# A recurrence's two heads in one row order, with the x term made ahead and the steps in a written order

## The chip, the cores and the metric

The kernel runs on one core of a Trainium2 chip. The metric is the device time of one execution in microseconds (us). Before the change, three executions took 2452.4, 2445.73 and 2456.51 us, so the median is 2452.4 us. The profile is of a further execution that took 2443.87 us.

Five engines work side by side, each through its own instructions in order: TensorE (PE in the profile, with its weight loads as PEld), VectorE (DVE), ScalarE (ACT), GpSimd (POOL) and SyncE (SP), which here does nothing but start DMAs. They wait for each other by semaphores.

## The reference, cut to what matters

One decoder block: RMSNorm, one input projection (1024 tokens, width 1024), a dilated attention branch and an RWKV-7 branch, a gated merge, an output projection, a SwiGLU feed-forward layer and a last RMSNorm. The change touches the RWKV-7 branch alone. It has 16 heads of 64 features and runs this recurrence over 1024 tokens:

```
def _rwkv7_step(state, inp):
    r_t, w_t, k_t, v_t, a_t, b_t = inp
    sa = jnp.einsum('bhvk,bhk->bhv', state, a_t)
    state = (state * w_t[:, :, None, :] + sa[..., None] * b_t[:, :, None, :]
             + v_t[..., None] * k_t[:, :, None, :])
    y = jnp.einsum('bhvk,bhk->bhv', state, r_t)
    return state, y
```

After it, y is normalized within each head, a bonus term is added, and the result is multiplied by a gate.

## The kernel before, in words

The recurrence is computed in chunks of L = 64 tokens. Within a chunk all products of two tokens come from one matmul and a triangular mask; a 64x64 triangular system is solved by the inverses of its 16x16 diagonal blocks; and only the state (64x64 per head) goes from chunk to chunk.

A **unit** is 256 tokens of four heads: 128 partitions hold two heads (rows 0 to 63 and 64 to 127), and the free axis holds two such pairs of 256 tokens, so a unit has NCH = 8 chunks, in two chains of four that advance together. There are 16 units. Each unit goes through:

- `rwkv_feat`: decay sums, their exponentials, normalized k.
- `rwkv_pre`: `ab` and `bk` (decayed operands); their products `pmg` (L730), masked on DVE into `aab` (L734) for one half of the rows, and copied by ACT (L736) and masked by POOL (L737) into `ab` for the other half; the first to memory and back, to fetch the diagonal blocks (`d1`, `a16`); v turned and copied twice, into `sv` and `uv` (L763, L764); the bonus; the block inverses on DVE (L786, L788), again to memory and back (`d2`, `cmp`), and spread by a mask multiply on POOL and DVE into `td` and `tdt` (L795); and then a row of small matmuls, each needing the last (`lvw` L807, `lvta`, `lvtt`, `lvw` L831, `lvt`), to the inverse `tt`.
- `rwkv_chain`: for each of four steps x (L868), u (L875) and the state update d (L887 on PE, L882 on POOL, four L891 on DVE), then the outputs `py`, and the normalization, gate and store.

The two heads of a pair use opposite row halves: a head's rows 0 to 63 hold its state and the other 64 its v, and the second head has them the other way round. So one 128-row matmul gives x with v's part in it:

```
T_.matmul(px[A, x, :], ab[:, cx, hh, 0, :], sv[:, cx, hh, :], start=True, stop=True)
```

All matmuls of the recurrence are small (64 or 32 columns, or 128) and on f32 operands; each stands as two records in the trace. The engine is kept fed between them by **filler**: the projection matmuls (L230, 128x512, one record each) of later heads' r, k, v and of the gates. `run` interleaves generators (chain, pre of the next unit, feat of the one after it, filler) by shares of a unit, one `yield` at a time. From that sequence, the compiler's list scheduler makes a fixed order for each engine, with durations that it assumes itself. What runs is this fixed order, and the waits in it are those of the chip.

Of the kernel before, what the change touches and what calls it, by code (L numbers as in the profile page):

```python
# [16 lines left out]
P = 128  # L17
S = 1024
# [8 lines left out]
NCH = HALF // L  # L27
NEG = -1.0e30
# [59 lines left out]
NV = 98  # L88

# [30 lines left out]
class K:  # L120
# [350 lines left out]
    def lora(self, sd, ad, gd):  # L471
# [9 lines left out]
        whh = sb.tile([P, 2, DM], F32R, tag="ab", name="whh", bufs=2)  # L481
# [52 lines left out]
    def rwkv(self, sd, ad, gd, ob, first, fill):  # L534

        nc, tc, a = self.nc, self.tc, self.a
        with ExitStack() as ctx:
# [17 lines left out]
            self.xm, self.svs, self.unit, self.feat = {}, {}, {}, {}  # L555
# [4 lines left out]
            run((chain_of([self.lora(sd, ad, gd), self.rwkv_gemm(0, "k"), self.rwkv_gemm(1, "k")]), 1, 0.0, 1.0))  # L560
            with tc.issue_after(self.last_sigmoid.ins):
                pre = nc.scalar.preload_act_table_set("natural_log_exp_and_others")
            with tc.issue_after(pre.ins):
                run((self.rwkv_feat(0, dd, "k"), 3, 0.1, 0.5), (self.rwkv_pre(0), 11, 0.6, 1.0), (self.rwkv_feat(1, dd), 3, 0.7, 1.0),
                    (chain_of([self.rwkv_gemm(0, "rv"), self.rwkv_gemm(1, "rv")]), 36, 0.0, 0.6),
                    (chain_of(gates(first)), 9 * len(first) + 1, 0.6, 1.0))
            later = [(q, x) for q in range(2, NPAIR) for x in "krv"]
            for n in range(N):
                ms = fill.get(n, ())

                k = 3 if n < 2 else 1 + n % 2
                f = [self.rwkv_gemm(*x) for x in later[:k]]
                later = later[k:]
                f += gates(ms)
                nf = 9 * len(f)
                jobs = [(self.rwkv_chain(n, gd, ob), 15, 0.0, 1.0)]
                if f:
                    jobs.append((chain_of(f), nf, 0.0, 1.0 if nf > 9 else 0.6))
                if n + 1 < N:
                    jobs.append((self.rwkv_pre(n + 1), 11, 0.0, 1.0))  # L580
                if n + 2 < N:
                    jobs.append((self.rwkv_feat(n + 2, dd), 3, 0.4, 1.0))
                run(*jobs)

    def rwkv_gemm(self, pr, kinds):
        nc, a, sb = self.nc, self.a, self.rb
        h = self.h
        for kind in kinds:
# [22 lines left out]
    def head_sums(self, src, nm):  # L611

# [4 lines left out]
        nc.vector.tensor_tensor(out=lo, in0=src, in1=hi, op=ALU.subtract)  # L617
        pss = self.rp.tile([P, HALF], F32, tag="st", name=f"pm{nm}", bufs=1)
# [15 lines left out]
    def block_of(self, d, n):  # L634

        pp, qd = n // 4, n % 4
        W = HALF // 2
        return d[2 * pp * P : (2 * pp + 2) * P, qd * W : (qd + 1) * W].rearrange("(x p) t -> p x t", x=2)

    def loaded(self, n, kinds):  # L640

        for x in kinds:
            t = self.xm[x, n] = self.rb.tile([P, HALF], F32, tag=f"xm{x}", name=f"xm{x}_{n}", bufs=2)
            self.nc.sync.dma_start(t.rearrange("p (x t) -> p x t", x=2), self.block_of(self.xd[x], n))

    def rwkv_feat(self, n, dd, kinds="krv"):

        nc, sb, ps = self.nc, self.rb, self.rp
        V, A_, T_ = nc.vector, nc.scalar, nc.tensor
        pp, qd = n // 4, n % 4  # L650
        nm = f"{pp}_{qd}"
        src = lambda d: self.block_of(d, n)
        f = lambda tag, bufs=1, shape=None: sb.tile(shape or [P, HALF], F32, tag=tag, name=f"{tag}_{nm}", bufs=bufs)
        pm = lambda n, shape=None: ps.tile(shape or [P, HALF], F32, tag="pm", name=f"pm{n}_{nm}", bufs=2)
        H0, H1 = slice(0, L), slice(L, P)
        heads = ((0, H0, H1), (1, H1, H0))
        col = lambda n, x: self.v(n, 2 * pp + x)
# [4 lines left out]
        xs = (slice(0, HALF // 2), slice(HALF // 2, HALF))  # L662
        halves = lambda t: t.rearrange("p (x t) -> p x t", x=2)
        nc.sync.dma_start(halves(sg), src(sd))
        nc.sync.dma_start(halves(at), src(ad))
# [14 lines left out]
        pss = self.head_sums(sq, f"ss_{nm}")  # L680
# [7 lines left out]
        for x, c in enumerate(xs):  # L688
            A_.activation(ka[:, c], at[:, c], AF.Identity, scale=col("k_a", x),
                          bias=self.oka[:, 2 * pp + x : 2 * pp + x + 1])  # L690
# [5 lines left out]
    def rwkv_pre(self, n):  # L696

        nc, sb, ps = self.nc, self.rb, self.rp
        V, A_, T_ = nc.vector, nc.scalar, nc.tensor
        pp, qd = n // 4, n % 4  # L700
        nm = f"{pp}_{qd}"
        src = lambda d: self.block_of(d, n)
# [3 lines left out]
        heads = ((0, H0, H1), (1, H1, H0))  # L706
        col = lambda n, x: self.v(n, 2 * pp + x)
        ch = lambda t: t.rearrange("p (c t) -> p c t", t=L)
        TT, STT, TS = V.tensor_tensor, V.scalar_tensor_tensor, V.tensor_scalar
        lv = lambda n, shape: ps.tile(shape, F32, tag="lv", name=f"lv{n}_{nm}", bufs=1)  # L710
# [3 lines left out]
        ab = f("ab", 2, [P, NCH, 2, 2, L])  # L714
        bk = f("bk", 1, [P, NCH, 2, L])
        for hh, A, _ in heads:
            STT(out=ab[A, :, hh, 0, :], in0=ch(kk)[A], scalar=-1.0, in1=pt[A, :, 0:L], op0=ALU.mult, op1=ALU.mult)
            TT(out=ab[A, :, hh, 1, :], in0=ch(r)[A], in1=pt[A, :, 1:], op=ALU.mult)
            TT(out=bk[A, :, hh, :], in0=ch(at)[A], in1=ch(pi)[A], op=ALU.mult)
            TT(out=bk[A, :, 1 - hh, :], in0=ch(k)[A], in1=ch(pi)[A], op=ALU.mult)  # L720

        yield

        aab = f("aab", 2, [P, NCH, 2, L])
        for q in range(2):
            q4 = slice(4 * q, 4 * q + 4)
            gs = [pm(f"g{q}{hh}", [P, 4, P]) for hh in range(2)]
            for j in range(4):
                for hh, A, _ in heads:
# [102 lines left out]
        for hh in range(2):  # L832
            A_.copy(w2[Q[2 * hh + 1]], pw[Q[2 * hh + 1]])
# [598 lines left out]
```

## Time and profile before

| | |
|---|---|
| median of three executions | 2452.4 us |
| profiled execution | 2443.87 us, of which the span of instructions is 2441.9 us |
| PE busy | 2331.3 us (95%) |
| DVE, ACT, POOL busy | 1600.6, 1202.7, 788.7 us |
| recurrence, 130 to 960 us after the start | 830 us, PE busy 775.03 us |

How to read it: busy time is the union of an engine's instructions, and matmuls overlap in the pipeline, so two matmuls that are 0.23 us apart can each be shown as 0.39 us long. The distance from start to start is what one costs. "Idle before" is the time the engine did nothing before an instruction, with the one that ended it. PEclk is the granted TensorE clock, where 1.00 is 2.4 GHz and half of it 1.2 GHz.

### The profile page before, as it was taken

The page shows a single profiled execution, that of the slowest core. Times are in us where ns is not written, and L with a number is a line of the kernel's source. Part 1 is how long each engine was busy: PE and PEld are TensorE (multiplying, and loading weights), DVE is VectorE, ACT ScalarE, POOL GpSimd, SP SyncE. Part 2 cuts the span into 40 slices and gives each one's busy share as a digit, 9 for nine tenths or more (in the row PEclk, how much of TensorE's full clock was granted, in tenths as well). Part 3 has the DMA queues.
Part 4 walks back from the last instruction along what each step waited for, and adds up shares of the span by engine and source line. Part 5 has one row for each costly group of instructions (what it writes and reads, how often), then busy time and mean ns, then how long its engine had stood idle before and what let it go on. Part 6 is the DMA issues. An engine that isn't in the chain of part 4 may idle for free. (4 is left out here: it accounts for less than half of the span.)

```text
span 2441.9 us, 40487 instructions
## 1 busy us (share of the span) xinstructions
PE 2331.3 (95%) x15102; PEld 1825.6 (75%) x15102; DVE 1600.6 (66%) x3251; ACT 1202.7 (49%) x2345; POOL 788.7 (32%) x689
## 2 busy tenths in 40 slices
PE   8999899999989999999999999999989999999998
PEld 5676677667666667777777777889968888887886
DVE  5267687888886773788888786342465555555656
ACT  7444455555445543677777775242233333334444
POOL 1133243334332432111111100023086777682200
PEclk9999999999999999999999999999989999999999
DMA  5642333323333322111111126453134444447555
GB/s 184 231 131 76 88 96 103 97 80 110 85 97 85 84 68 89 35 36 39 40 39 40 39 68 222 149 188 119 70 103 151 147 154 170 165 164 264 183 190 184
DMA packets 302532, 284.79 MB, mean 117 GB/s; under 512 B 82411, under 2 KB 226240, under 8 KB 302208
## 3 DMA queue, kind: packets, MB, share of 16 engines
q1 hardware_dynamic: 297856, 267.10, 34.9%
q0 software_dynamic: 4480, 15.12, 1.7%
q8 instruction: 118, 1.93, 0.3%
q14 instruction: 78, 0.64, 0.1%
HBM read 187.65 MB, written 92.54 MB: 115 GB/s over the span
## 5 line engine op out<-in xcount | busy, mean ns | idle before, releaser
L426 ACT CAST ph<-pt 128x512 fp32r<-128x512 f32 x192 | 89.8, 478 | 75.0 <-PE pt L423 74.4
L427 DVE TENSOR_TENSOR pl<-pt,ph 128x512 fp32r<-128x512 f32 x192 | 106.1, 554 | 31.3 <-ACT ph L426 29.9
L737 POOL TENSOR_TENSOR ab<-ab,gmask 64x512 f32<-64x512 f32 x64 | 91.3, 1427 | 105.4 <-ACT ab L736 100.1
L1315 PE MATMUL o<-dwlo,dfh 128*128 128x512 f32 x276 | 109.7, 398 | 2.9 <-DVE dwlo L1082 2.9
L423 PE MATMUL pt<-ident,pb 128*128 128x128 f32 x576 | 103.9, 277 | 8.0 <-DVE pb L400 5.6
L230 PE MATMUL pg_sg<-hhi,wh_sg 128*128 128x512 f32 x256 | 110.8, 433 | 0.0
L1315 PE MATMUL o<-dwhi,dfh 128*128 128x512 f32 x276 | 109.3, 396 | 1.5 <-ACT dwhi L1081 1.5
L882 POOL TENSOR_TENSOR s<-sv,pt 64x128 f32<-64x128 f32 x120 | 59.8, 498 | 153.8 <-DVE sv L891 144.2
L1315 PE MATMUL o<-dwhi,dfl 128*128 128x512 f32 x276 | 109.1, 395 | 0.0
L397 ACT ACTIVATE pb<-pb,mn 128x128 f32<-128x128 f32 (+7 forms) x128 | 99.2, 777 | 19.1 <-DVE mn L392 17.4
L1082 DVE TENSOR_TENSOR dfl<-fr,dfh 128x512 fp32r<-128x512 f32 x69 | 58.5, 851 | 71.9 <-ACT dfh L1081 71.7
L230 PE MATMUL pg_sg<-hhi,wl_sg 128*128 128x512 f32 x256 | 105.0, 410 | 0.0
L230 PE MATMUL pg_sg<-hlo,wh_sg 128*128 128x512 f32 x256 | 104.0, 406 | 0.0
L423 PEld LDWEIGHTS pt<-ident,pb 128*128 128x128 f32 x576 | 71.0, 141 | 36.9 <-DVE pb L400 8.8
L891 DVE SCALAR_TENSOR_TENSOR sv<-chd,pt,s 64x64 f32<-64x64 f32 x240 | 67.9, 283 | 41.2 <-PE chd L887 35.7
L1081 ACT CAST dfh<-fr 128x512 fp32r<-128x512 f32 x69 | 42.6, 618 | 97.7 <-PE o L1315 85.0
L209 POOL TENSOR_TENSOR wl_sg<-wr_sg,wh_sg 128x512 fp32r<-128x512 f32 x32 | 44.9, 1402 | 112.4 <-ACT wh_sg L208 106.5
L392 DVE CUSTOM_DVE_ANT_0 pb<-sc,nbias 128x512 f32<-128x512 f32 (+3 forms) x128 | 72.6, 585 | 7.7 <-PE sc L390 6.4
L1017 PE MATMUL wo<-wowoh,mhi 128*128 128x256 f32 x256 | 72.5, 284 | 1.0 <-DVE x L1020 1.0
L432 PE MATMUL po<-ph,vt 128*128 128x512 f32 x192 | 72.8, 383 | 0.4 <-ACT ph L426 0.3
L1017 PE MATMUL wo<-wowoh,mlo 128*128 128x256 f32 x256 | 72.5, 283 | 0.0
L1017 PE MATMUL wo<-wowol,mhi 128*128 128x256 f32 x256 | 72.3, 283 | 0.0
(502 smaller groups left out, 7578.1 us busy)
## 6 DMA issues: line engine op xcount, KB each, us to landing
fr<-fd SPq DMA_DIRECT2D x77, 256.0 KB
wd<-in_ffn_w_down_dram SPq DMA_DIRECT2D x11, 1024.0 KB
td<-wd SPq DMA_DIRECT2D x11, 1024.0 KB
wr<-td SPq DMA_DIRECT2D x44, 256.0 KB
wg<-in_ffn_w_gate_dram SPq DMA_DIRECT2D x10, 1024.0 KB
wu<-in_ffn_w_up_dram SPq DMA_DIRECT2D x10, 1024.0 KB
fd<-fs SPq DMA_DIRECT2D x40, 256.0 KB
wr<-in_ffn_w_down_dram SPq DMA_DIRECT2D x33, 256.0 KB
```

What stands on the lines that cost most here:

```text
L230: nc.tensor.matmul(pg, lw, rx[:, k, :], start=(i == 0), stop=(i == n - 1))
L392: nc.vector.tensor_tensor_reduce(out=pb[:, b * HALF : b * HALF + n], in0=sc[:, :n], in1=nbias[:, bo : bo + n], scale=1.0, scalar=(3.0e38 i ...
L397: nc.scalar.activation(pb[:, :nk], pb[:, :nk], AF.Exp, bias=last, scale=-1.0, accum_out=mn[:, 2:3])
L423: nc.tensor.transpose(pt[:, j * P : (j + 1) * P], probs[j][:, kb * P : (kb + 1) * P], self.ident)
L426: nc.scalar.copy(ph[:, c0:], pt[:, c0:])
L427: nc.vector.tensor_tensor(out=pl[:, c0:], in0=pt[:, c0:], in1=ph[:, c0:], op=ALU.subtract)
L432: nc.tensor.matmul(po[:, c0:], vt[:, b, hh, :], ph[:, c0:], start=(b == 0), stop=False)
L737: nc.gpsimd.tensor_tensor(out=dst, in0=dst, in1=m4[B], op=ALU.mult)
L882: nc.gpsimd.tensor_tensor(out=s2[A], in0=sv[A, c::NC, hh, :], in1=pt[A, c::NC, L : L + 1].broadcast_to([L, 2, L]), op=ALU.mult)
L891: STT(out=nsv[A, ncx, hh, :], in0=pd[A, x, :], scalar=pt[A, cx, L : L + 1], in1=s2[A, x, :], op0=ALU.mult, op1=ALU.add)
L1017: nc.tensor.matmul(pt, lw[:, k, ts_], rx[:, k, :], start=(n == 0), stop=(n == 3 * KT - 1))
L1315: T_.matmul(pt, lw[:, ts_], rx, start=(first and n == 0 and x == 0), stop=(last and x == 2), skip_group_check=True)
```

## The change

The row order becomes the same for both heads. g (all masked products) is kept on 128 partitions per head: b's rows in 0 to 63 and k's in 64 to 127, masked by one DVE instruction of 128 rows, and neither ACT nor POOL takes part. The state `st` is a tile of its own with head 0 in rows 0 to 63 and head 1 in the others. Hence:

- x is a 64-row matmul of the state alone; v's part of it, `xv`, is made ahead in `rwkv_pre` (16 small matmuls a unit, one ACT copy), and DVE adds it instead of ACT's copy of x.
- The old state enters the update as a matmul with the identity (16 a unit), and one DVE multiply by the decay ends it, in place of POOL's product and four DVE instructions.
- The block inverses go to memory straight into the places of a zeroed 64x64 layout (pieces of 64 bytes) and come back as `td` and `tdt`; the mask multiplies on POOL and DVE are gone. The masked products are also read back whole (`aa`). The zeroes are written once, by eight DMAs at the start.
- The bonus and the end of a unit become generators of their own, sums over heads are split in two (operands in one step, matmuls in the next), and `ALONG` says which of them advances after each of the 12 steps of a chain. The last step of `rwkv_pre` moves into the next unit.

The diff, cut to its core:

```
-                jobs = [(self.rwkv_chain(n, gd, ob), 15, 0.0, 1.0)]
...
+                run((self.unit_steps(n, own), 12, 0.0, 1.0), (chain_of(f), nf, 0.0, 1.0))
...
+    ALONG = (("last", "pre"), ("pre",), ("pre",), ("pre", "out"), ("out", "pre"), ("pre",), ("pre", "feat"),
+             ("pre", "feat"), ("feat",), ("pre", "feat"), ("pre", "bonus"), ("pre", "bonus"))
+    def unit_steps(self, n, own):
+        chain = self.rwkv_chain(n)
+        for along in self.ALONG:
+            next(chain, None)
+            for x in along:
+                if own[x] is not None:
+                    next(own[x], None)
+            yield
...
+                for i in range(2):
+                    flat = d[i].rearrange("(p f) -> p f", p=P)
+                    nc.sync.dma_start(flat[:, :HALF], zero)
+                    nc.sync.dma_start(flat[:, HALF:], zero[:, : flat.shape[1] - HALF])
...
-            for hh, A, B in heads:
-                TT(out=aab[A, q4].rearrange("p j i t -> p j (i t)"), in0=gs[hh][A], in1=m4[A], op=ALU.mult)
-                dst = ab[B, q4, hh].rearrange("p j i t -> p j (i t)")
-                A_.copy(dst, gs[hh][B])
-                nc.gpsimd.tensor_tensor(out=dst, in0=dst, in1=m4[B], op=ALU.mult)
+            for hh, A in heads:
+                TT(out=g[:, q4, hh].rearrange("p j i t -> p j (i t)"), in0=gs[hh], in1=m4, op=ALU.mult)
...
+        for hh, A in heads:
+            nc.sync.dma_start(aa[A], mats(d1)[hh].rearrange("c (s t) -> s c t", t=L))
...
-            for hh, _, B in heads:
-                A_.copy(sv[B, par::2, hh, :], pv[src, :, hh, :])
-                A_.copy(uv[B, par::2, hh, :], pv[src, :, hh, :])
+            A_.copy(uv[H1, par::2], pv[src])
...
+        for c in range(NCH):
+            for hh, A in heads:
+                T_.matmul(pv[A, c, :], g[H1, c, hh, 0, :], uv[H1, c, hh, :], start=True, stop=True)
+        A_.copy(xv, pv)
...
-        for i, (dst, eng) in enumerate(((td, nc.gpsimd), (tdt, nc.vector))):
-            cmp_ = f(f"cmp{i}", 1, [P, NCH, 16])
-            nc.sync.dma_start(cmp_, d2[i].rearrange("(c x) i j -> (x i) c j", c=NCH))
-            eng.tensor_tensor(out=dst, in0=cmp_.unsqueeze(2).broadcast_to([P, NCH, 4, 16]),
-                              in1=self.blk16.unsqueeze(1).unsqueeze(3).broadcast_to([P, NCH, 4, 16]), op=ALU.mult)
+        for i, dst in enumerate((td, tdt)):
+            nc.sync.dma_start(diag(d2[i]), tp[:, i])
+            m2 = mats(d2[i].rearrange("(c x) -> c x", c=NCH))
+            for hh, A in heads:
+                nc.sync.dma_start(dst[A], m2[hh].rearrange("c (s t) -> s c t", t=L))
...
-                    T_.matmul(px[A, x, :], ab[:, cx, hh, 0, :], sv[:, cx, hh, :], start=True, stop=True)
-            A_.copy(xt, px)
+                T_.matmul(px[A, x, :], ar[A, cx, 0, :], st[A, cx, :], start=True, stop=True)
+            V.tensor_tensor(out=xt, in0=px, in1=xv[:, c::NC, :], op=ALU.add)
...
-                        STT(out=nsv[A, ncx, hh, :], in0=pd[A, x, :], scalar=pt[A, cx, L : L + 1], in1=s2[A, x, :],
-                            op0=ALU.mult, op1=ALU.add)
+                    T_.matmul(pd[A, x, :], self.ident[:, A], st[:, cx, :], start=True, stop=False)
+                    T_.matmul(pd[A, x, :], bkt[:, cx, A], uv[:, cx, hh, :], start=False, stop=True)
+                nst, c1 = (st, c + 1) if c < NC - 1 else (self.svs[n + 1], 0)
+                V.tensor_tensor(out=nst[:, c1::NC, :], in0=pd,
+                                in1=pt[:, c::NC, L : L + 1].broadcast_to([P, UP, L]), op=ALU.mult)
```

In the engines' orders, three places show what moves. The first is PE's order around the first matmuls of the triangular solve of the third unit, `lvw` (names end in head pair and quarter; `pg_sv3` is filler). Before:

```order
L230 MATMUL pg_sv3_0_2632<-hlo0_169,wh_sv3_1_2628 128x512
L807 MATMUL lvw_0_2_2602<-td_0_2_2545,am_0_2_2599 64x64 x16
L230 MATMUL pg_sv3_0_2632<-hhi0_168,wl_sv3_1_2629 128x512
L230 MATMUL pg_sv3_0_2632<-hhi0_168,wh_sv3_1_2628 128x512
L230 MATMUL pg_sv3_0_2632<-hlo0_169,wh_sv3_1_2628 128x512
L230 MATMUL pg_sv3_0_2632<-hhi0_168,wl_sv3_1_2629 128x512
L230 MATMUL pg_sv3_1_2726<-hhi1_250,wh_sv3_0_2622 128x512
L816 MATMUL lvta_0_2_2653<-am_0_2_2599,tdt_0_2_2546 32x32 x16
```

And the same place of the changed kernel:

```order
L840 MATMUL lvw_0_2_2671<-td_332,am_0_2_2476 64x64
L239 MATMUL pg_sv3_1_2640<-hhi1_250,wh_sv3_0_2554 128x512
L239 MATMUL pg_sv3_1_2640<-hlo1_251,wh_sv3_0_2554 128x512
L239 MATMUL pg_sv3_1_2640<-hhi1_250,wl_sv3_0_2555 128x512
L239 MATMUL pg_sv3_1_2640<-hhi1_250,wh_sv3_1_2560 128x512
L239 MATMUL pg_sv3_1_2640<-hlo1_251,wh_sv3_1_2560 128x512
L239 MATMUL pg_sv3_1_2640<-hhi1_250,wl_sv3_1_2561 128x512
L239 MATMUL pg_sv3_1_2640<-hhi1_250,wh_sv3_1_2560 128x512
L840 MATMUL lvw_0_2_2671<-td_332,am_0_2_2476 64x64 x15
```

The 16 matmuls are split: the first stands alone, since it needs one of `td`'s two reads only, and seven filler matmuls stand ahead of the other 15.

The second is SP's order where a unit's block inverses (`t16`) go to memory and come back. Before:

```order
L205 DMA wr_sg4_1_7487<-in_w_in_dram 128x4x128
L790 DMA d2_2_1_6441<-t16_2_1_6575 64x2x256
L794 DMA cmp0_2_1_6613<-d2_2_1_6441 128x8x16
L794 DMA cmp1_2_1_6616<-d2_2_1_6441 128x8x16
L665 DMA at_3_0_7770<-ad_73 128x2x256
```

And of the changed kernel:

```order
L214 DMA wr_sg4_0_7371<-in_w_in_dram 128x4x128
L828 DMA d2_1_335<-t16_2_1_6478 64x16x16 x2
L831 DMA td_332<-d2_1_335 64x8x64 x2
L831 DMA tdt_333<-d2_1_335 64x8x64 x2
L643 DMA gates_75<-gt3_1_6693 128x512
```

One write and two reads become two writes (in pieces of 16 numbers) and four reads, back to back.

The third is DVE's order from a copy of u to the new state. Before, with the steps of the block inverses between:

```order
L786 TENSOR_TENSOR t16m_1_0_3705<-a16_1_0_3571,t16_1_0_3704 64x11x5
L891 SCALAR_TENSOR_TENSOR sv_0_3_3025<-chd2_0_3_3773,pt_0_3_2564,s2_0_3_3770 64x64
L788 TENSOR_TENSOR t16_1_0_3704<-t16_1_0_3704,t16m_1_0_3705 64x11x5
L891 SCALAR_TENSOR_TENSOR sv_0_3_3025<-chd2_0_3_3773,pt_0_3_2564,s2_0_3_3770 64x64
L786 TENSOR_TENSOR t16m_1_0_3705<-a16_1_0_3571,t16_1_0_3704 64x10x6
L891 SCALAR_TENSOR_TENSOR sv_0_3_3025<-chd2_0_3_3773,pt_0_3_2564,s2_0_3_3770 64x64
```

And of the changed kernel:

```order
L927 COPY uv_0_3_3027<-chu0_0_3_3452 64x2x64
L769 TENSOR_TENSOR g_1_0_3490<-pmg01_1_0_3492,gmask_319 128x4x128
L937 TENSOR_TENSOR st_0_3_3026<-chd0_0_3_3479,pt_0_3_2535 128x2x64
L920 TENSOR_TENSOR xt_0_3_3515<-chx1_0_3_3510,xv_0_3_3057 128x128
L769 TENSOR_TENSOR g_1_0_3490<-pmg10_1_0_3517,gmask_319 128x4x128
```

Four state instructions, with other work between them, become one; the sum that makes `xt` is new on this engine.

## Rows read from the trace of the kernel before

**Rows 1.** The page: the span, and PE's busy time.

```profile
span 2441.9 us, 40487 instructions
...
PE 2331.3 (95%) x15102; PEld 1825.6 (75%) x15102; DVE 1600.6 (66%) x3251; ACT 1202.7 (49%) x2345; POOL 788.7 (32%) x689
```

**Rows 2.** Busy time by stretch: length; PE, PEld, DVE, ACT, POOL; clock; DMA.

```profile
130.00:960.00 830.00, 775.03 (x7660) 568.51 (x7659) 636.06 (x1446) 411.30 (x867) 298.48 (x321) 0.98 0.33 91
960.00:1600.00 640.00, 620.96 (x3074) 496.18 (x3073) 464.90 (x1094) 413.51 (x825) 76.14 (x61) 0.99 0.24 75
```

**Rows 3.** What PE waited for, 130 to 960: total us, times, longest.

```profile
PE lvw L807 <- POOL td L795: 21.9, 12, 3.1
PE chu L875 <- ACT tt L840: 6.4, 4, 2.9
PE chx L868 <- DVE sv L891: 5.5, 10, 1.3
PE pmbk L769 <- ACT uv L764: 4.9, 3, 2.3
PE pmvar L620 <- DVE hsl_var L617: 3.0, 4, 0.9
PE pmvar L619 <- ACT hsh_var L616: 2.4, 3, 1.1
```

**Rows 4.** Timeline of PE near 387: start, us, instruction, records, idle before.

```profile
386.26 0.39 PE L230 MATMUL pg_sk<-hlo,wh_sk 128*128 128x512 f32 x1
386.50 0.39 PE L230 MATMUL pg_sk<-hhi,wl_sk 128*128 128x512 f32 x1
386.81 0.45 PE L868 MATMUL chx<-sv,ab 128*64 128x64 f32 x8
387.20 0.51 PE L230 MATMUL pg_sk<-hhi,wh_sk 128*128 128x512 f32 x1
388.45 1.15 PE L807 MATMUL lvw<-td,am 64*64 64x64 f32 x32 [0.75 <-POOL td L795]
389.53 0.50 PE L230 MATMUL pg_sk<-hlo,wh_sk 128*128 128x512 f32 x1
389.87 0.40 PE L230 MATMUL pg_sk<-hhi,wl_sk 128*128 128x512 f32 x1
```

**Rows 5.** Timeline of PE near 225: 128*64 and then 64*64.

```profile
225.05 0.28 PE L900 MATMUL py<-ab,sv 128*64 128x64 f32 x2
225.26 0.50 PE L902 MATMUL py<-aab,uv 64*64 64x64 f32 x9
```

**Rows 6.** Timeline of PE near 236: matmuls on row halves, 64*128.

```profile
235.53 1.16 PE L730 MATMUL pmg<-ab,bk 64*128 64x128 f32 x8
236.62 0.56 PE L807 MATMUL lvw<-td,am 64*64 64x64 f32 x12
```

**Rows 7.** Timeline of all engines, 382 to 388: block inverses to memory and back.

```profile
382.34 0.59 SPq L790 DMA_DIRECT2D d<-t  x1
...
384.95 0.99 SPq L794 DMA_DIRECT2D cmp<-d  x2
...
387.36 1.04 POOL L795 TENSOR_TENSOR td<-cmp,blk 128x512 f32<-128x512 f32 x1 [0.54 <-PE chx L868]
```

**Rows 8.** Groups by line, 130 to 960: busy us, mean ns; idle before.

```profile
L737 POOL TENSOR_TENSOR ab<-ab,gmask 64x512 f32<-64x512 f32 x64 | 91.3, 1427 | 105.4 <-ACT ab L736 100.1 <-issue 3.1
L891 DVE SCALAR_TENSOR_TENSOR sv<-chd,pt,s 64x64 f32<-64x64 f32 x240 | 67.9, 283 | 41.2 <-PE chd L887 35.7 <-POOL am L800 1.5
L882 POOL TENSOR_TENSOR s<-sv,pt 64x128 f32<-64x128 f32 x118 | 59.0, 500 | 148.7 <-DVE sv L891 144.2
L764 ACT COPY uv<-pmvt 64x256 f32<-64x256 f32 x64 | 23.4, 366 | 0.2
```

**Rows 9.** Timeline of SP, 0 to 60: the gap where the zeroes go.

```profile
24.95 0.43 SPq L554 DMA_DIRECT2D blk<-in_c_blk_dram  x1
30.59 0.58 SPq L478 DMA_DIRECT2D w<-in_decay_w_dram  x1
```

More of the change, by code (lines that the diff above doesn't have):

```diff
@@ L581, in rwkv @@
[L581 to L585, printed above, removed]
+                nf += 9 * len(ms)
+                pres[n + 1], bons[n + 1] = self.rwkv_pre(n + 1), self.rwkv_bonus(n + 1)
+                feats[n + 2], outs[n] = self.rwkv_feat(n + 2, dd), self.rwkv_out(n, gd, ob)
+                own = {"last": pres.get(n), "pre": pres[n + 1] if n + 1 < N else None, "bonus": bons[n + 1] if n + 1 < N else None,
+                       "feat": feats[n + 2] if n + 2 < N else None, "out": outs.get(n - 1)}
@@ L586, in rwkv_gemm @@
+    def rwkv_gemm(self, tiles):
         nc, a, sb = self.nc, self.a, self.rb
         h = self.h
-        for kind in kinds:
+        for pr, kind in tiles:
             i0 = {"r": 0, "k": 8, "v": 16}[kind]
@@ L661, in rwkv_feat @@
         sg, at = f("sg"), f("at", 2)
[L662 to L665, printed above, removed]
+        xs = [slice(x * UW, (x + 1) * UW) for x in range(UP)]
+        nc.sync.dma_start(by_pair(sg), self.block_of(sd, n))
+        nc.sync.dma_start(by_pair(at), self.block_of(ad, n))
         self.loaded(n, kinds)
@@ L757, in rwkv_pre @@
+        for b in range(2):
+            pk = pm(f"bk{b}", [P, 4, P])
+            for x in range(4):
+                T_.transpose(pk[:, x, :], flat(bk[:, 4 * b + x]), self.ident)
+            A_.copy(bkt[:, 4 * b : 4 * b + 4, :], pk)
+        st = sb.tile([P, NCH, L], F32, tag="sv", name=f"st_{nm}", bufs=2)
+        self.svs[n] = st
+        if n % NQ == 0:
+            nc.gpsimd.memset(st[:, 0::NC, :], 0.0)
         uv = f("uv", 2, [P, NCH, 2, L])
@@ L895, in rwkv_chain, with outputs @@
-        for part in range(2):
+        qd = n % NQ
+        nm = f"{n // NQ}_{qd}"
+        H0, H1 = slice(0, L), slice(L, P)
+        heads = ((0, H0), (1, H1))
+        ar, g, tt, st, uv, xv, bkt, pt = (self.unit[n][x] for x in "ar g tt st uv xv bkt pt".split())
+        py = self.py[n] = ps.tile([P, HALF], F32, tag="py", name=f"py_{nm}", bufs=1)
+        cp = lambda n, shape: ps.tile(shape, F32, tag="ch", name=f"ch{n}_{nm}", bufs=1)
+        def outputs(part):
             for c in range(NCH):
-                for hh, A, _ in heads:
+                for hh, A in heads:
@@ L903, in rwkv_chain @@
                                   skip_group_check=True)
-            yield
-        sq = f("sy")
+        for c in range(NC):
+            every = [(x, x * NC + c, hh, A) for x in range(UP) for hh, A in heads]
+            px = cp(f"x{c}", [P, UP, L])
+            for x, cx, hh, A in every:
+                T_.matmul(px[A, x, :], ar[A, cx, 0, :], st[A, cx, :], start=True, stop=True)
+            xt = sb.tile([P, UP, L], F32, tag="xt", name=f"xt_{nm}", bufs=1)
+            V.tensor_tensor(out=xt, in0=px, in1=xv[:, c::NC, :], op=ALU.add)
+            if c == NC - 1:
+                outputs(0)
+            yield
+            pu = cp(f"u{c}", [P, UP, L])
+            for x, cx, hh, A in every:
+                T_.matmul(pu[A, x, :], tt[A, cx, :], xt[A, x, :], start=True, stop=True)
+            V.tensor_copy(uv[H0, c::NC, 0, :], pu[H0])
+            A_.copy(uv[H0, c::NC, 1, :], pu[H1])
+            yield
+            if not (qd == NQ - 1 and c == NC - 1):
+                pd = cp(f"d{c}", [P, UP, L])
+                for x, cx, hh, A in every:
+                    T_.matmul(pd[A, x, :], self.ident[:, A], st[:, cx, :], start=True, stop=False)
[3 more added lines that the diff above has]
+                                in1=pt[:, c::NC, L : L + 1].broadcast_to([P, UP, L]), op=ALU.mult)
+            if c == NC - 1:
+                outputs(1)
+            yield
```

246 lines of the change are left out of this document (112 added, 134 removed).

## The prediction

> **What bounds the kernel now.** I read the page first: TensorE is busy 2331.3 of 2441.9 us, every other engine far less [rows 1]. So a change gains only where TensorE stands idle or runs slowly, and loses where it gives TensorE more to do. The busy time by stretches shows where the idle time is: the recurrence, 130 to 960 us, has 830 us with 775.03 busy, so 55 us idle, at a mean granted clock of 0.98. The attention behind it loses 19 us in 640 [rows 2]. The reader is to see two losses in the recurrence: 55 us of idle time, and 2% of 830 us, some 17 us, of cycles that the clock did not grant; 72 us together. That is the most that better spacing of the steps can bring, whatever it saves on other engines.
>
> Then the list of what TensorE waited for: 21.9 us for `td` (the block inverses, spread by a mask multiply on POOL), 6.4 for the finished inverse `tt`, 5.5 for the new state, 4.9 for ACT's copies of v, 5.4 for the operands of the head sums of the output [rows 3]. The other 11 us are waits of 2.2 us and less.
>
> Last, the timeline, for what a small matmul costs. Filler matmuls start 0.24 us apart. Four `chx` matmuls (8 records) take 0.39 us to the next start, sixteen `lvw` matmuls 1.08 [rows 4]: 0.0575 us for each further one. The rest is the price of leaving the filler and coming back: 0.31 instead of 0.24 before, 0.39 less 0.23 within, 0.34 instead of 0.23 after; 0.35 us for each stretch of small matmuls.
>
> **The change part by part.** On TensorE it adds:
> - xv: 8 chunks by 2 heads by 16 units, 256 matmuls, 14.7 us. Bounds: 128 columns on row halves (`pmg`) take 1.09 us for four, about 0.24 each without the entry of some 0.15 [rows 6], so half of that, 0.12, if the two heads of `xv` (same rows, other columns) do not run side by side: 31 us. Below 14.7 I see no reason. I take 14.7, since `chx` also has two heads that differ in columns alone.
> - The identity: 240 matmuls (16 per unit, 15 of every 16 steps), 13.8 us. Here two matmuls for the same columns follow each other. If that ends the overlap, these and the 240 behind them cost 0.12 instead of 0.0575 each: 44 us instead of 13.8. I take 13.8, the spacing that `chx` and `lvw` both have, since the pairs of the two heads still alternate.
> - Entries: in the built order there are 335 stretches of small matmuls between filler before and 308 after, so 27 fewer by 0.35 us, 9.4 us saved, in spite of split groups such as `lvw`.
> - Changes between tile shapes inside a stretch: a 128x64 matmul (two records) ahead of a 64x64 one takes 0.21 us to the next start [rows 5] instead of 0.0575, so 0.15 more. There are 92 in the order before and 163 after, as x and the first outputs become 64x64 and the second outputs 128x64: 10.7 us more.
>
> The sum on TensorE is 14.7 + 13.8 - 9.4 + 10.7, some 30 us more work. That is larger than I expected from a change that takes so much off the other engines, and it decides the case: the 72 us of losses must shrink by more than 30.
>
> What goes elsewhere: POOL's masking of g (91.3 us) and its product for the state (59.0) [rows 8]; the `td` multiply; half of ACT's copies of v and all of its copies of g; of the state's four DVE instructions of 0.283 us per step [rows 8] three, so 0.85 us off each of the 63 links of the chain, while the sum for xt (I estimate 0.28 from the same row; ACT's copy goes) costs about nothing there. None of this is on the path by itself, since these engines are idle for 23% of the stretch (DVE, 636.06 of 830) or more [rows 2]; it counts by the waits that it ends. Term by term:
> - `td`, 21.9 us, 1.37 per unit. Today the write is issued at 382.34, the reads at 384.95, POOL starts at 387.36 and takes 1.04 [rows 7]; TensorE gets `td` 6.1 us after the write. In the change the first read's data are used as they land, 5.0 us after it if 64-byte pieces cost no more; then 0.33 per unit stay, 5 us. I take 7, since the second half and `tdt` come later, behind seven fillers of 0.23 us or more.
> - The head sums' 5.4 us: operands and matmuls are a step apart now. The state's 5.5: one DVE instruction and no POOL. ACT's copies, 4.9: fewer. The 6.4 for `tt`: the last step is moved ahead of the next u, but as long a chain leads to it; I keep 4. With the rest, 33 us become 11.
> - The clock: I let its 17 us go with the idle time, 18/55 of it staying, 6.
>
> Idle time from 55 to 18 and the clock's from 17 to 6: 48 us less. Against 30 us more, 18 us gained.
>
> What is late next: `tdt` and the chain of small matmuls to `tt`, where the order has less filler between steps than before.
>
> SP gets 11 small DMAs per unit where it had 6, and waits in line for their landing; behind it are weight loads. Weights are loaded ahead, into three buffers; without that cover the 5 more would cost their issue, 0.5 us each [rows 7], 40 us. I take 0. The eight DMAs of zeroes stand at the start where SP has nothing to do from 25.4 to 30.59 [rows 9]; at 0.5 us each they fit. Otherwise they cost 4 us.
>
> The Trainium skill, in TensorEngine Tiling (Array Packing), section Tiling Modes, says that tiles of the array are independent and run matmuls and weight loads in parallel. Rows do not bear that out for row halves: `pmg` with two halves is no faster than its columns in turn [rows 6]. By the rule `xv` would be as cheap as I took it; by `pmg`'s row it costs 16 us more.
>
> **The rivals.**
> 1. *The waits move instead of going.* The built order is dense by assumed durations; each unit still has two trips to memory and a row of dependent matmuls. For it: `td`'s wait is a wait for the landing first, and POOL's multiply only 1.04 of 6.1 us. Against it: the splits. If idle time falls to 33 and the clock's part to 11, that is 28 off against 30: 2 us slower, 2454.
> 2. *The trip through memory gets longer.* The inverses are written in 64-byte pieces and read by four DMAs in place of two. If the four reads land one after the other, as the first does now, 2.4 us each, and PE's order has them closer, `td`'s second half is ready 2.6 + 2 x 2.4 = 7.4 us after the write, 1.3 later than today, in all 16 units: `td`'s wait grows from 21.9 to 43. With the others' 11 that is 54 us idle and 17 for the clock, so 1 off against 30 on: 29 slower, 2481. It decides from the point where idle time and clock together stay above 42 us. Against it: the two reads of today are issued within 0.99 us and a single wait covers both [rows 7]. The Trainium skill, in DMA: Bandwidth & Descriptors, section Specifications, says that transfers below 512 bytes are done as read-modify-write; no row here shows a 64-byte write.
> 3. *The identity and xv do not overlap in columns.* 30 + 16 us more than in the first case: 28 slower, 2480. Against it: every row of two heads so far overlaps.
> 4. *The change does what it says and all waits go:* 72 - 30, 42 us gained, 2410; I count it to the first case.
>
> **How the numbers follow.** The profiled execution took 2443.87 us, 8.5 less than the median of 2452.4; I take differences from the median. Most likely, with 0.46: 18 us gained, 2434, with its own range 2410 to 2442. Rival 1: 0.27. Rival 2: 0.18. Rival 3: 0.09. Half a per cent, 12 us, is about what can be told from no change. Faster by more is the first case, 0.46. Within it is rival 1 and a few of the others: 0.29. Slower: 0.25. The range takes in the first case and rival 1 and reaches some way towards the others, which need only part of their price: 2408 to 2476.
>
> **What would show it.** Right: idle time of TensorE in the recurrence falls below 25 us, `lvw`'s wait below 10; busy time there rises by some 25; `chd` with eight matmuls takes about 0.62 us to the next start, `xv`'s sixteen 1.08; the clock is at 0.99; POOL is below 600 us. Wrong: waits of `lvw`, `lvta` or `lvtt` for a DMA above 20 us together (rival 2); eight `chd` matmuls above 0.85 us (rival 3); new waits for xt on DVE, or for `tt` at the start of a unit (rival 1); or a stretch of attention that changes by more than 5 us, which I expect not to change.

## The result and the profile after

The changed kernel took 2414.75 us (median of four executions, 2413.4 to 2419.28), the kernel before 2454.45: a ratio of the means of 0.9848, 95% interval 0.9819 to 0.9877. Between the medians 39.7 us were gained where 18 were forecast: the direction was right, the gain was more than twice as large, inside the range. The two profiled executions differ by less, 2443.87 against 2413.52.

The page of the changed kernel, its span and the busy time of each engine (answers to [rows 1]):

```profile
span 2411.8 us, 41914 instructions
...
PE 2332.9 (97%) x16094; PEld 1839.9 (76%) x16094; DVE 1462.7 (61%) x3055; ACT 1131.9 (47%) x2137; POOL 620.0 (26%) x486
```

TensorE is as busy as before, with 992 records more. To see why, the recurrence has to be cut at the same events in both kernels: from the first `pmg` to the last small matmul and the head sums behind it. First the kernel before (columns as in [rows 2]):

```profile
151.90:955.80 803.90, 748.93 (x7546) 547.37 (x7546) 617.79 (x1417) 399.51 (x847) 292.78 (x317) 0.97 0.32 89
```

And the changed kernel:

```profile
157.20:926.40 769.20, 748.97 (x8535) 559.79 (x8535) 482.24 (x1225) 327.58 (x639) 126.96 (x116) 0.99 0.40 107
```

The stretch is 34.7 us shorter. Its busy time is the same; its idle time (length less busy) falls from 55.0 to 20.2. It begins 5.3 us later (157.2 for 151.9), and all that follows is shorter by 0.7: the span by 30.1.

What TensorE waited for, 130 to 960 us of the changed kernel (answers to [rows 3]):

```profile
PE py L911 <- DVE uv L927: 9.4, 12, 1.9
PE chu L926 <- DVE xt L920: 6.1, 13, 0.9
PE ptv L318 <- ACT vv L329: 4.0, 1, 4.0
PE chd L934 <- ACT uv L928: 1.1, 1, 1.1
PE pg_v L239 <- ACT qk_k L354: 1.0, 1, 1.0
PE pmbk L791 <- DVE g L769: 1.0, 1, 1.0
PE pmg L766 <- DVE g L769: 0.8, 3, 0.3
```

The old list is gone: no head sums, no state, `td` below the list's end with 0.6. Two waits are new, `py` for DVE's copy of u and `chu` for the sum that makes `xt`. (`ptv` and `pg_v` stand in the attention behind the recurrence, which has the same two waits in the kernel before.)

Now the small matmuls, TensorE near 240 and 254 us (answers to [rows 4, 6]):

```profile
239.05 0.34 PE L934 MATMUL chd<-st,ident 128*64 128x64 f32 x4
239.22 0.29 PE L935 MATMUL chd<-uv,bkt 128*64 128x64 f32 x4
239.33 0.33 PE L934 MATMUL chd<-st,ident 128*64 128x64 f32 x4
239.45 0.33 PE L935 MATMUL chd<-uv,bkt 128*64 128x64 f32 x4
239.71 1.16 PE L766 MATMUL pmg<-ar,bk 64*128 64x128 f32 x16
240.80 0.50 PE L239 MATMUL pg_sv<-hhi,wh_sv 128*128 128x512 f32 x1
...
254.66 1.15 PE L809 MATMUL pmxv<-uv,g 64*64 64x64 f32 x32
255.74 0.51 PE L239 MATMUL pg_sr<-hhi,wh_sr 128*128 128x512 f32 x1
```

The eight `chd` matmuls of a step, four of them with the identity, take 0.66 us to the next start, sixteen of `xv` 1.08: the prices that were forecast. But `pmg` has changed: 16 records, eight matmuls, take 1.09 us, the same as the 8 records, four matmuls, of [rows 6]. The group as a whole shows it, `pmg` of the kernel before, 130 to 960 us (busy us, mean ns | idle before):

```profile
L730 PE MATMUL pmg<-ab,bk 64*128 64x128 f32 x512 | 67.0, 291 | 4.5 <-ACT ab L736 1.8 <-DVE bk L720 1.2 <-DVE t L788 0.9
```

and of the changed kernel:

```profile
L766 PE MATMUL pmg<-ar,bk 64*128 64x128 f32 x512 | 47.8, 295 | 0.8 <-DVE g L769 0.8
```

The same number of records, each as long as before, and 19.2 us less of TensorE: they overlap. What moved is their order. Both kernels write the two heads in turn; in the built order of the kernel before most stand four and four, in the changed one in turn (`pmg00` is the first head, in rows 0 to 63, `pmg01` the second):

```
before  L730 MATMUL pmg00_0_2_2293<-ab_0_2_2251,bk_0_2_2252 128x128 x4
        (seven fillers)
        L730 MATMUL pmg01_0_2_2294<-ab_0_2_2251,bk_0_2_2252 128x128 x4
after   L766 MATMUL pmg00_0_2_2290<-ar_0_2_2228,bk_0_2_2229 128x128
        L766 MATMUL pmg01_0_2_2291<-ar_0_2_2228,bk_0_2_2229 128x128
        L766 MATMUL pmg00_0_2_2290<-ar_0_2_2228,bk_0_2_2229 128x128
        L766 MATMUL pmg01_0_2_2291<-ar_0_2_2228,bk_0_2_2229 128x128
        (and twice more in turn)
```

Counted over the orders, 35 pairs stand in turn before and 114 after, of 128.

Last the start, where the zeroes go (answers to [rows 9]). SP of the changed kernel, the first and last of the eight, and a load of weights behind them:

```profile
25.93 0.43 SPq L563 DMA_DIRECT2D blk<-in_c_blk_dram  x1
32.16 0.33 SPq L572 DMA_DIRECT2D d<-td  x1
...
36.05 0.43 SPq L573 DMA_DIRECT2D d<-td  x1
...
54.98 0.38 SPq L214 DMA_DIRECT2D wr_sr<-in_w_in_dram  x1
```

and the one longer wait of TensorE in its first 130 us that the kernel before does not have:

```profile
PE pg_sr L239 <- ACT wh_sr L217: 3.3, 1, 3.3
```

The zeroes do not stand in the gap, which ended at 30.59 in [rows 9], but behind it, from 32.16, and the weights of the first r come late.

### The profile page after: what moved, and what is told of

Same layout as the page of the kernel before. It is cut to its first block, busy times and chain, and to the rows that moved or that the text cites. A ratio compares the mean times of both kernels' runs of the same rounds, so it can differ in the third digit from the quotient of the medians.

```text
span 2411.8 us, 41914 instructions
## 1 busy us (share of the span) xinstructions
PE 2332.9 (97%) x16094; PEld 1839.9 (76%) x16094; DVE 1462.7 (61%) x3055; ACT 1131.9 (47%) x2137; POOL 620.0 (26%) x486
## 5 line engine op out<-in xcount | busy, mean ns | idle before, releaser
L822 DVE TENSOR_TENSOR t<-t,t16m 64x15 f32<-64x15 f32 (+7 forms) x240 | 77.9, 325 | 5.0
L442 PE MATMUL po<-pl,vt 128*128 128x512 f32 x192 | 67.9, 361 | 0.9 <-DVE pl L436 0.9
L928 ACT COPY uv<-chu 64x128 f32<-64x128 f32 x64 | 16.8, 263 | 108.7 <-DVE uv L927 108.0
```

What stands on the lines that cost most here:

```text
L442: nc.tensor.matmul(po[:, c0:], vt[:, b, hh, :], pl[:, c0:], start=False, stop=(b == nkb - 1))
L822: TT(out=t16[:, j + 1 :, :m_], in0=t16[:, j + 1 :, :m_], in1=tm[:, :n_, :m_], op=ALU.add)
```

## The experiments

The kernels were timed four at a time, in the order of the table, each group beside its own runs of the kernel before (medians 2454.17, 2454.48, 2448.13), so kernels of different groups are compared by their ratio to it. The changed kernel stands at 0.9848.

| kernel | median us | ratio to before, interval |
|---|---|---|
| a_heads_apart | 2429.94 | 0.9904 [0.9887, 0.9920] |
| a_add_dve | 2392.3 | 0.9744 [0.9726, 0.9762] |
| a_td_mask | 2409.57 | 0.9821 [0.9797, 0.9844] |
| a_old_steps | 2535.24 | 1.0331 [1.0310, 1.0351] |
| a_g_old | 2421.59 | 0.9867 [0.9841, 0.9893] |
| a_one_sum | 2415.63 | 0.9846 [0.9819, 0.9874] |
| best_zero | 2386.37 | 0.9719 [0.9693, 0.9745] |
| best_mask | 2396.95 | 0.9767 [0.9736, 0.9798] |
| best_turn | 2368.94 | 0.9680 [0.9660, 0.9699] |
| best_py | 2367.59 | 0.9671 [0.9651, 0.9690] |
| a_even | 2407.85 | 0.9836 [0.9814, 0.9858] |
| best_maskpy | 2411.37 | 0.9845 [0.9818, 0.9873] |

**a_heads_apart.**

```diff
-            for j in range(4):
-                for hh, A in heads:
+            for hh, A in heads:
+                for j in range(4):
                     T_.matmul(gs[hh][:, j, :], flat(bk[A, 4 * q + j]), flat(ar[A, 4 * q + j]), start=True, stop=True)
```

> The changed kernel with one edit: the products pmg are written head by head, four and four, where they took turns between the heads. In TensorE's order 29 pairs still stand in turn, where the changed kernel has 114 and the kernel before 35. Theory A (two matmuls on opposite row halves run side by side when they stand in turn; this is the part of the gain that the forecast left out): 85 pairs fewer by 0.22 us, 19 us slower than the changed kernel, about 2434; the pmg group's busy time goes from 47.8 to about 65 us. Rival B (row halves never overlap, the gain over the forecast comes from better spacing): within 3 us of the changed kernel, 2412 to 2418, and pmg's busy time about as it is.

0.57% slower than the changed kernel by the ratios, some 14 us (15 between the medians), with `pmg` of this run at:

```profile
L766 PE MATMUL pmg<-ar,bk 64*128 64x128 f32 x512 | 66.2, 291 | 0.2 <-DVE g L769 0.2
```

Theory A. Nothing else was changed in the source, the filler matmuls in the recurrence are as many, and this group takes 18 us more.

**a_add_dve.**

```diff
-                    T_.matmul(pd[A, x, :], self.ident[:, A], st[:, cx, :], start=True, stop=False)
-                    T_.matmul(pd[A, x, :], bkt[:, cx, A], uv[:, cx, hh, :], start=False, stop=True)
+                    T_.matmul(pd[A, x, :], bkt[:, cx, A], uv[:, cx, hh, :], start=True, stop=True)
...
+                sm = sb.tile([P, UP, L], F32, tag="xt", name=f"sm_{nm}", bufs=1)
+                V.tensor_tensor(out=sm, in0=pd, in1=st[:, c::NC, :], op=ALU.add)
-                V.tensor_tensor(out=nst[:, c1::NC, :], in0=pd,
+                V.tensor_tensor(out=nst[:, c1::NC, :], in0=sm,
```

> The changed kernel without the identity matmuls: the state enters by a sum on DVE (128x128) ahead of the multiply by the decay. Theory A (the identity is 16 us of TensorE work and the chain of steps has room for one more DVE instruction of 0.28 us per step): 16 us faster than the changed kernel, 2399, with DVE's busy time up by some 18 us and no wait of chx for the state above 3 us together. Rival B (the links of the chain are what TensorE waits for): the waits of chx for the state come back, 5 to 20 us, the time is 2410 to 2425.

1.06% faster than the changed kernel by the ratios, 26 us (22 between the medians). TensorE's busy time fell from 2332.9 to 2315.4 us. The waits of this run, 130 to 930 us:

```profile
PE py L911 <- DVE uv L927: 5.1, 8, 1.8
PE ptv L318 <- ACT vv L329: 3.7, 1, 3.7
PE chu L926 <- DVE xt L920: 3.1, 4, 0.9
PE lvw L840 <- DMA td<-d: 2.2, 4, 0.8
PE pmbk L791 <- DVE g L769: 1.2, 1, 1.2
PE chx L918 <- DVE st L938: 1.0, 2, 0.7
```

Theory A, and more than its 16 us: the chain has room for another DVE instruction in each step (`chx` waits 1.0 us for the state), and the waits of `py` and `chu` are 7 us shorter. The identity, one of the change's parts, costs time.

**a_td_mask.** td and tdt as in the kernel before, by compact reads and mask multiplies; the zeroes and their layout are left out.

```diff
-            nc.sync.dma_start(diag(d2[i]), tp[:, i])
...
-            for hh, A in heads:
-                nc.sync.dma_start(dst[A], m2[hh].rearrange("c (s t) -> s c t", t=L))
...
+            nc.sync.dma_start(cmp_, d2[i].rearrange("(c x) i j -> (x i) c j", c=NCH))
+            eng.tensor_tensor(out=dst, in0=cmp_.unsqueeze(2).broadcast_to([P, NCH, 4, 16]),
+                              in1=self.blk16.unsqueeze(1).unsqueeze(3).broadcast_to([P, NCH, 4, 16]), op=ALU.mult)
```

> The changed kernel with td and tdt made as before: the inverses go to memory in one piece per row, come back compact by two reads, and a mask multiply on POOL and on DVE spreads them. Theory A (the new layout in memory took the wait of 21.9 us away): lvw waits 10 to 20 us for POOL and DVE again, 2425 to 2435. Rival B (the order of steps took it away, by putting work between the reads and lvw): lvw waits below 5 us, and the time is within 5 us of the changed kernel.

The wait comes back as theory A has it:

```profile
PE lvw L836 <- POOL td L825: 15.2, 13, 1.9
```

and the time does not: 0.27% below the changed kernel, with overlapping intervals. So neither theory as written. The new layout does end the wait, and it costs as much: TensorE's busy time is 2313.2 us here, 19.7 below the changed kernel's, and between 130 and 930 us the three groups that read `td` and `tdt` (`lvw`, `lvta`, `lvtt`) are busy for 18.8, 11.1 and 18.4 us here and for 24.3, 14.6 and 23.1 there, 13.7 us more. The zeroes are gone too: the first `pmg` starts at 154.0 us, not at 157.2. What it is in those groups, best_turn below shows.

**a_old_steps.** The arithmetic of the changed kernel, mixed by shares.

```diff
-                run((self.unit_steps(n, own), 12, 0.0, 1.0), (chain_of(f), nf, 0.0, 1.0))
...
+                jobs = [(chain_of([self.rwkv_chain(n)] + ([outs[n]])), 14, 0.0, 1.0)]
...
+                    jobs.append((chain_of(f), nf, 0.0, 1.0 if nf > 9 else 0.6))
...
+                    jobs.append((chain_of([pres[n + 1], bons[n + 1]]), 14, 0.0, 1.0))
...
+                    jobs.append((feats[n + 2], 4, 0.4, 1.0))
+                run(*jobs)
```

> The changed kernel with its steps mixed by shares as in the kernel before: chain and end of a unit are one sequence, pre and bonus one, feat in the last 0.6, and no step of pre moves into the next unit. All the arithmetic is that of the changed kernel. TensorE's order has 264 stretches of small matmuls (309 in the changed kernel, 336 before) and 70 pairs of pmg in turn (114). Theory A (the written order ends the waits): waits of TensorE in the recurrence come back to 30 to 45 us in place of some 20, 16 us are saved by fewer stretches, 10 lost by pmg: 2415 to 2435. Rival B (the lighter engines end the waits, whatever the order): waits as in the changed kernel, about 2409.

Both times were wrong by 100 us or more. In the waits theory A is nearer; the longest entry, 130 to 930 us:

```profile
PE lvw L845 <- DMA td<-d: 31.4, 13, 11.8
```

So the new layout ends the wait for `td` only together with the written order: theory B falls. Most of the time lost lies at the end. TensorE in two stretches of the recurrence (length, busy, clock, DMA):

```profile
130.00:900.00 770.00, 737.93 (x7479) 0.98 0.39 106
900.00:1070.00 170.00, 104.35 (x1259) 0.61 0.17 42
```

The last 170 us have 104 busy, at a clock of 0.61, not far from the lower level: the filler was used up early (none of it starts between 900 and 1058 us), and the last units stand with their small matmuls alone. Since this mix is not that of the kernel before either (bonus and the end of a unit stand elsewhere), its 2535 us are not the price of the old order.

**a_g_old.** The mask of g in two halves, the lower on ACT and POOL.

```diff
-                TT(out=g[:, q4, hh].rearrange("p j i t -> p j (i t)"), in0=gs[hh], in1=m4, op=ALU.mult)
+                dst = g[:, q4, hh].rearrange("p j i t -> p j (i t)")
+                TT(out=dst[H0], in0=gs[hh][H0], in1=m4[H0], op=ALU.mult)
+                A_.copy(dst[H1], gs[hh][H1])
+                nc.gpsimd.tensor_tensor(out=dst[H1], in0=dst[H1], in1=m4[H1], op=ALU.mult)
```

> The changed kernel with the mask of g in two halves, as before: rows 0 to 63 by one DVE instruction, rows 64 to 127 copied by ACT and masked by POOL, 64 times each. Theory A (work on ACT and POOL off the path is worth nothing by itself, as the forecast has it): POOL's busy time is some 90 us higher, TensorE's waits are those of the changed kernel, the time 2410 to 2420. Rival B (the longer way to g, some 1.4 us of POOL behind a copy, stands in front of pmbk, pmxv or the first trip to memory): TensorE waits for POOL's g by 8 us or more together, or for what depends on it, and the time is 2423 to 2435.

0.19% slower, inside the intervals; between the two. Its new waits in the trace are small:

```profile
PE lvw L843 <- DMA td<-d: 3.2, 3, 1.5
PE pmbk L794 <- ACT g L771: 3.1, 1, 3.1
PE pmg L766 <- ACT g L771: 1.5, 3, 0.9
```

Masking on 128 partitions at once takes 64 instructions each off ACT and POOL. It gains some 5 us by the ratios, 7 between the medians, which the intervals do not tell from nothing.

**a_one_sum.**

```diff
-        parts = self.head_parts(sq, f"var_{nm}")
         yield
+        parts = self.head_parts(sq, f"var_{nm}")
```

(and the same for the bonus and the norm of k)

> The changed kernel with operands and matmuls of each sum over heads in one step again (bonus, variance, norm of k); the number of steps and all arithmetic stay. Theory A (the split ended the 5.4 us that TensorE waited for these operands): the waits of pmvar, pmbonus and pmss for hsh and hsl come back with 4 to 8 us, and the time is 2419 to 2423. Rival B (the order between the steps hides them either way): these waits stay below 2 us, and the time is within 3 us of the changed kernel.

No change, and no wait for `hsh` or `hsl` in its list. Rival B: with the steps in their new order those operands are early either way, and the split of the sums ended nothing.

**best_zero.** a_add_dve with the zeroes issued by POOL (`nc.gpsimd.dma_start`).

> The kernel with the sum on DVE in place of the identity (2392.3), and the eight DMAs of zeroes at the start issued by POOL instead of SP. Theory A (on SP they hold up the loads behind them: the first pmg starts at 157.2 us with them and at 154.0 in the run without them): 3 us faster, 2389, first pmg at about 155. Rival B (it is the transfers themselves, 3 MB or so beside the first weights, that cost): no change, 2390 to 2394, first pmg at 158.

0.26% below a_add_dve with intervals that overlap, so by time alone unclear; in the trace the first `pmg` starts at 153.2 us for 158.0, and the wait of `pg_sr` is gone. Theory A. The transfers are still there, though smaller than the expectation has it: the trace shows four of 256 KB and four of 4 KB, 1.04 MB together.

**best_mask.** a_add_dve with a_td_mask, td on DVE and tdt on POOL.

> The kernel with the sum on DVE in place of the identity (2392.3), and the inverses brought back compact and spread by mask multiplies as in the run with td made as before, but with the engines exchanged: td, needed first, on DVE and tdt on POOL. Theory A (POOL's 1.04 us for td are most of the 15.2 us that lvw waits there; on DVE they are about half; stretches of small matmuls 293 in place of 309): lvw waits below 8 us, no zeroes at the start, 2379 to 2385. Rival B (DVE is busy with other instructions when the read lands, or lvta then waits for POOL): 15 us of waits stay, 2386 to 2392.

```profile
PE lvw L836 <- DVE td L825: 17.9, 13, 2.5
```

Rival B in the wait, which is as long on DVE, although its multiply is shorter (a median of 0.69 us, against 1.29 on POOL in a_td_mask). DVE stood idle for 21.0 us before it until the reads had landed, so most of the wait seems to be the trip through memory; the two parts were not separated. The time, 0.24% above a_add_dve with overlapping intervals, lies beyond both theories.

**best_turn.** best_zero, with the second head first in the three groups that read td and tdt.

```diff
-            for hh, A in heads:
+            for hh, A in heads[::-1]:
                 T_.matmul(pw[A, c, :], am[A, c, :], td[A, c, :], start=True, stop=True)
```

(and the same in `lvta` and `lvtt`)

> The kernel with the sum on DVE and the zeroes issued by POOL (2386.4), with the second head written first in lvw, lvta and lvtt, so that the first matmul already needs the read that lands last and the group isn't split. Stretches of small matmuls 309 to 295. Theory A (each stretch costs 0.35 us of TensorE, as in the forecast's term for entries): 5 us faster, 2381, with the waits of lvw for DMA at most 2 us higher. Rival B (the whole group now stands and waits for the last read, in all 16 units): lvw waits above 8 us, 2386 to 2394.

0.40% faster than best_zero, some 10 us; the trace has 16. The groups in best_zero:

```profile
370.12 0.33 PE L840 MATMUL lvw<-td,am 64*64 64x64 f32 x2 [0.59 <-DMA td<-d]
...
371.95 1.14 PE L840 MATMUL lvw<-td,am 64*64 64x64 f32 x30
...
373.83 0.24 PE L849 MATMUL lvta<-am,tdt 32*32 32x32 f32 x2
374.00 0.33 PE L856 MATMUL lvtt<-tdt,am 64*64 64x64 f32 x2
...
375.33 0.69 PE L849 MATMUL lvta<-am,tdt 32*32 32x32 f32 x30
375.95 1.14 PE L856 MATMUL lvtt<-tdt,am 64*64 64x64 f32 x30
```

and in best_turn:

```profile
369.25 1.15 PE L840 MATMUL lvw<-td,am 64*64 64x64 f32 x32
...
372.08 0.69 PE L849 MATMUL lvta<-am,tdt 32*32 32x32 f32 x32
372.71 1.15 PE L856 MATMUL lvtt<-tdt,am 64*64 64x64 f32 x32
```

The recurrence to its last `chx`, best_zero:

```profile
153.00:895.00 742.00, 728.01 (x8007) 540.12 (x8007) 488.64 (x1283) 325.51 (x636) 129.19 (x116) 1.00 0.42 110
```

and best_turn:

```profile
153.00:877.50 724.50, 711.84 (x8001) 532.53 (x8002) 489.71 (x1282) 325.62 (x636) 126.96 (x116) 1.00 0.43 113
```

16.2 us less busy, for the same matmuls, and no wait in exchange (`lvw` waits 0.3 us for `td`, 2.5 in best_zero). By their lines, 130 to 930 us, `lvw`, `lvta` and `lvtt` are busy for 23.4, 14.9 and 23.5 us in best_zero and for 18.4, 11.1 and 18.4 in best_turn: 13.9 us of it is in the split groups themselves. By the forecast's term 14 stretches by 0.35 would be 5 us; the rest may lie in the changes of tile shape between the pieces, which was not separated. These are the same groups, and nearly the same sum, as in a_td_mask: that is the price that the two reads of td laid on the changed kernel.

**best_py.** best_turn, and the outputs with the chunks of the last step at the end: `for c in (*range(NC - 1), *range(NC, NCH - 1), NC - 1, NCH - 1)`.

> As best_turn, and the second outputs py written with the two chunks of the last step at the end, so that the other six don't stand behind DVE's late copy of u. Stretches 295 to 280. Theory A: 15 stretches by 0.35 us and the 5 us that py waits for DVE's uv: 7 to 10 us faster than best_turn, about 2373. Rival B (these matmuls need that copy at the same place in any order, and the wait only moves to the last two chunks): 5 us from the stretches alone at most, 2376 to 2381, py's wait stays at 4 us or more.

No faster than best_turn: the intervals overlap. Rival B, with its sign:

```profile
PE py L911 <- DVE uv L927: 7.0, 11, 2.0
```

Nor did the 15 stretches less show as 5 us: TensorE is busy for 2297.5 us, 2297.4 in best_turn. So 0.35 us a stretch is no general price. With best_turn this is the fastest kernel: 0.9671 of the kernel before, 1.8% below the changed kernel.

**a_even.**

```diff
-    ALONG = (("last", "pre"), ("pre",), ("pre",), ("pre", "out"), ("out", "pre"), ("pre",), ("pre", "feat"),
-             ("pre", "feat"), ("feat",), ("pre", "feat"), ("pre", "bonus"), ("pre", "bonus"))
+    ALONG = (("last", "out", "pre"), ("out", "pre"), ("pre",), ("pre", "feat"), ("pre",), ("pre", "feat"), ("pre",),
+             ("pre", "feat"), ("pre",), ("pre", "feat"), ("pre", "bonus"), ("bonus",))
```

> The changed kernel with another written order of steps: the end of the last unit runs in steps 1 and 2, where it ran in 4 and 5, pre goes one step in each of the first eleven, feat in every second one, bonus in the last two. TensorE's order has 284 stretches and 104 pairs of pmg in turn (309 and 114 in the changed kernel). Theory A (what ends the waits is that a unit's steps are spread evenly over the chain's steps; which steps meet matters little): waits of TensorE below 30 us, 9 us less for the stretches, 2 more for pmg, 2405 to 2420. Rival B (it is the exact places; the run mixed by shares took 2535): 2430 and above, with waits of lvw for td or of pmvar above 20 us.

0.12% below the changed kernel, no difference, with waits of 16 us in the list of this run, 130 to 930 us. Theory A: this even spread does as well. Others were not run.

**best_maskpy.** a_add_dve with a_td_mask and the order of outputs of best_py.

> The kernel with the sum on DVE, the order of outputs of best_py, and td and tdt made by mask multiplies as before (POOL and DVE), without zeroes. 279 stretches, as in best_py. Theory A (the layout in memory is worth nothing on balance: lvw's wait of some 15 us for POOL stands against splits and zeroes that the layout costs, and best_py has neither): 8 to 15 us slower than best_py. Rival B (POOL's wait of 15 us is mostly time that TensorE gets back elsewhere): within 4 us of best_py.

```profile
PE lvw L836 <- POOL td L825: 24.8, 14, 3.3
```

44 us slower than best_py in the same group; A's direction, three times its size. Beside the wait the mean clock was 0.980 to 0.990 in its five runs, 0.991 to 0.994 in best_py's. Of 2411 us, a clock lower by 0.007 is at most 17 us (an estimate, if time goes fully with the clock). Without splits the layout in memory is worth its place: in the changed kernel it was not. How much it is worth is less sure: best_mask, with td on DVE and the outputs in the old order, is 0.90% behind best_turn, some 21 us.

## Why the prediction was half the gain

Point by point:

- **The sum on TensorE, +30, was the step that failed.** Busy time of the recurrence did not rise; with the clock's 11 us taken off, I had +19. `pmg` is the 19 that is missing: 67.0 to 47.8. I costed it at no change and wrote that "`pmg` with two halves is no faster than its columns in turn". The row behind that, [rows 6], holds four matmuls of one head (the built order has them as `pmg01` four times, ahead of `lvw`), and I took it for two heads. A busy sum of 67.0 over 256 matmuls, 0.26 each, said only that most did not overlap, and the built orders said why. a_heads_apart shows the mechanism. The Trainium skill, TensorEngine Tiling (Array Packing), section Tiling Modes, says that tiles run matmuls in parallel; the row at 239.71 agrees for row halves, and what I set against the rule was my misreading.
- xv (14.7) and the identity (13.8) were sized right: 1.08 for sixteen, 0.66 for eight with their shape change. Rival 3 falls. That the identity would also lengthen waits was not in the sum: without it the kernel is 22 to 26 us faster (a_add_dve).
- **Idle time, 55 to 18:** measured 20.2. But not by the terms I gave. `td` fell to 0.6, not 7, and `tt` to 0.7, not 4; the split sums did nothing (a_one_sum); two new waits, 9.4 and 6.1, took the room. Rival 1 named that kind of wait, and a place for one, `xt` on DVE.
- **Rival 2 falls.** Its sign was waits for a DMA above 20 us; `lvw` waits 0.6. Near 371 the write of 64-byte pieces is issued at 371.09 and the first read at 373.76, 2.67 us later, against 2.61 before [rows 7]. SP issues two other DMAs between the two, so the write itself may have been quicker:

```profile
371.09 1.31 SPq L828 DMA_DIRECT2D d<-t  x2
...
373.76 1.37 SPq L831 DMA_DIRECT2D td<-d  x2
375.22 1.26 SPq L831 DMA_DIRECT2D tdt<-d  x2
```

- **The clock, 11 us, was too small, because one profile had to stand for the kernel.** The profiled execution had a mean clock of 0.985; the 29 of the experiments have 0.973 to 0.984, median 0.980, and the slower ones the lower clocks (2471.18 us at 0.973, 2441.96 at 0.984). If time goes fully with the clock, the loss at 0.980 is some 49 us (2% of 2452), at the changed kernel's 0.990 some 24: 25 us from the clock in a usual run, 14 more than forecast. That is an upper estimate. A straight line through the 29 executions has only 16 us for 0.010 of clock, which is 5 more than forecast. I saw that the profile was 8.5 us faster than the median, and did not ask what it was faster in.
- The zeroes: "otherwise they cost 4 us" was the case; best_zero shows the start 4.8 us earlier.
- POOL at 620.0, not below 600: my own rows gave 788.7 less 91.3, 59.0 and 16 by 1.04, that is 622.
- Attention did not change: 593.9 us from `ptv` to the projection behind it before, 592.6 after.

Together: 18 forecast, 19 for `pmg`, 5 to 14 for the clock, less 2 of idle time and less 5 at the start, is 35 to 44, against 39.7 measured. One term is missing in it: `lvw` (its first group), `lvta` and `lvtt`, busy for 50.2 us before and 62.0 after, 130 to 960 us, whose splits the forecast priced by their entries alone.

What stays open: why a_old_steps runs out of filler where the kernel before, also mixed by shares, does not; how the price of a split group divides between its entries and its shapes; and why the waits of `py` and `chu` shrink by 7 us when the identity goes.

## What to carry to other kernels

Cost a group of matmuls from its busy total over its count, and look in the built order how its members stand before a single row is taken for the group: the order of two heads was worth 14 us of time, 18 of TensorE's, here with no instruction added. Where a tile is filled by two reads, try beginning with the matmul that needs the later one: here the other order split the group, at 0.40%. And on an engine 95% busy, work that is moved onto it to relieve an idle engine (the identity, 22 to 26 us with its waits) has to be paid by waits that are really there.

## What the runs showed of the hardware

- f32 matmuls of 128 columns on opposite row halves run side by side when they stand in turn, into different tiles of PSUM: 1.09 us for eight, against 1.09 for four of one half.
- The clock is a spread between executions of one kernel, not a number: 0.973 to 0.984 for the kernel before, and some 29 us of time between the ends. best_py has it higher and narrower (0.991 to 0.994), best_maskpy, where `lvw` waits 24.8 us, lower (0.980 to 0.990). That waits of that kind lower the clock is not shown: a_td_mask, where `lvw` waits 15.2 us, has 0.990 to 0.993.
